# Six heads projected with the modulation, shift_m by stationary weights, latent attention beside the output product

## The chip, the cores and the metric

The kernel runs on one core of a Trainium2 chip. The metric is the device time of one execution in microseconds (us). Before the change the median of three runs is 2721.38 us (2719.5 to 2721.91).

## The reference, cut to what matters

Two transformer blocks work on 256 rows of width 2048. The change touches the first block up to the end of its output product:

```python
mod = silu(c) @ w_ada + b_ada                       # 2048 x 12288
shift_m, scale_m, gate_m, shift_f, scale_f, gate_f = split(mod, 6)
h = modulate(rmsnorm(x, g_norm_mix), shift_m, scale_m)
dq, dk, dv, q_lat, kv_lat, k_pe = split(h @ w_in)   # 8 heads x 384 columns, 512, 256, 64
o_diff = rmsnorm(softmax(q1 k1) v - lam * softmax(q2 k2) v, g_diff_sub) * 0.8   # 8 heads of 128
q = rmsnorm(q_lat, g_q_a) @ w_q_b                   # 8 heads x (128 + 64 rotated)
k_nope, v_mla = split(rmsnorm(kv_lat, g_kv_a) @ w_kv_b)   # 8 heads x (128, 128)
o_mla = softmax(q [k_nope, rope(k_pe)]) @ v_mla
x = x + gate_m * (concat(o_diff, o_mla) @ w_out)
h = modulate(rmsnorm(x, g_norm_ffn), shift_f, scale_f)    # the feed-forward part follows
```

Everything is float32. The feed-forward part of the block and the whole second block are untouched.

## The kernel before, in words

**The weight stream.** `make_plan` writes one list of tiles, each at most 128x1024 float32 (two row blocks by 512 columns; 384 KB for a difference head). SyncE's DMA queue loads them in the order of the list into 8 raw buffers (6, and 2 more; from block j = 2 of the output product on only the 6). `split_next` takes the next tile. A *main* tile, a weight of a matrix product, is split in two parts: ScalarE rounds the high part `wh` and VectorE forms the rest `wl` (both in `split`, L119 and L120). Four split tiles can wait (`ahead` says how many are wanted). A *side* tile is a piece of `w_ada`: it goes to `ada_part`, where VectorE multiplies it by silu(c) and sums along the row (L224). Only `shift_m` goes to TensorE there: two matmuls of 512 columns with one column of silu(c) as weights (L208) add to one row of 512 sums, and after 8 tiles ScalarE copies the row (L212) and four matmuls of one element (L215) turn it into a column.

**The products.** `linear` takes a split tile and issues 12 matmuls for it (`mm3`, L134 to L136: high by high, high by low, low by high, for two row blocks of the result and two row blocks of the weight). After each tile it ticks the *fillers*: generators with the attention heads' steps (and some others), of which a tick advances at most two. `ensure` and `drain` advance fillers with no product between them.

**The order of the first block.** `block1_attention_proj` takes the 2048 features in four quarters: the modulation of a quarter (8 tiles of `scale_m`, 8 of `shift_m`), then of that quarter q_lat, kv_lat and difference head 0, whose results stay in PSUM over all four quarters. Then head 1, q's and k/v's latent products (L573 to L627 with `cq_gen`, `ckv_gen`, `qr_gen`). `block1` then projects heads 2 to 7 while the steps of `mla_head` and `diff_head` run as fillers. It waits for all latent heads and four difference heads, splits their results into `OT`, and multiplies by w_out: blocks j = 0 and 1 with the first six of eight groups of features, the remaining attention, the last two groups, and then j = 2 and 3. Side tiles of `gate_m`, `scale_f` and `shift_f` are spread between: 24 over 28 main tiles, 48 over the next 48, and 8 over the last 22.

In `diff_head` the row norm of a head's result takes its reciprocal root on GpSimd (12 instructions of 128x1, L98 and L100); ScalarE then scales the result `on` (L736) and TensorE transposes it.

Of the kernel before, what the change touches and what calls it, by code (L numbers as in the profile page):

```python
# [42 lines left out]
class Kernel:  # L43
    def __init__(self, ctx, tc, a, out, offs):
# [9 lines left out]
        gap.tile([P, 88], F32, name="gap")  # L54
# [144 lines left out]
    def ada_part(self, e, src):  # L199

        v = self.nc.vector
        sec, k = e["sec"], e["k"]
        if e["kind"] == "ada_pe":
            if k == 0:
                self.ada_row = self.trp()
            for kk in range(2):
                kt = k * 2 + kk
                self.nc.tensor.matmul(self.ada_row[0:1, :], lhsT=self.silu_c[:, kt:kt + 1],  # L208
                                      rhs=src[:, kk * 512:(kk + 1) * 512], start=kt == 0, stop=kt == 15)
            if k == 7:  # L210
                row = self.junkp.tile([P, 512], F32, tag="junk", name="row")[0:1]
                self.nc.scalar.activation(row, self.ada_row[0:1, :], AF.Copy)  # L212
                ps = self.trp()
                for i in range(4):
                    self.nc.tensor.matmul(ps[:, i:i + 1], lhsT=row[:, i * P:(i + 1) * P], rhs=self.ones[0:1, 0:1],  # L215
                                          start=True, stop=True)
                c = slice(e["j"] * 4, e["j"] * 4 + 4)
                v.tensor_add(self.mod[sec][:, c], ps[:, 0:4], self.s("b_" + sec)[:, c])
                self.done.add((sec, e["j"]))
            return  # L220
        junk = self.adap.tile([P, 1024], BF16, tag="ajunk", name="ajunk", bufs=1)
        if k == 0:
            self.ada_sum = self.tiny("ada_sum", 8)
        v.scalar_tensor_tensor(junk, src, 1.0, self.silu_row[:, (k % 2) * 1024:(k % 2 + 1) * 1024],  # L224
                               op0=OP.mult, op1=OP.mult, accum_out=self.ada_sum[:, k:k + 1])
        if k == 7:
            c = slice(e["j"] * 4, e["j"] * 4 + 4)
            dst = self.mod[sec][:, c]
            h = self.ada_sum.rearrange("p (i h) -> p i h", h=2)
            v.tensor_add(dst, h[:, :, 0], h[:, :, 1])  # L230
            v.tensor_add(dst, dst, self.s("b_" + sec)[:, c])
            if sec.startswith("scale"):
                gain = self.s("g_norm_mix" if sec == "scale_m" else "g_norm_ffn")[:, c]
                v.scalar_tensor_tensor(dst, dst, 1.0, gain, op0=OP.add, op1=OP.mult)
            self.done.add((sec, e["j"]))
# [210 lines left out]
    def block1_attention_proj(self):  # L446
        nc, v = self.nc, self.nc.vector
        es = ExitStack()
        keep = es.enter_context(self.tc.tile_pool(name="mla", bufs=1))
        qn = keep.tile([P, 8, T], F32, name="qn")  # L450
        kn = keep.tile([P, 8, T], F32, name="kn")
        vm = keep.tile([P, 2, 1024], F32, name="vm")
        qr = keep.tile([P, 4, T], F32, name="qr")
        kr = keep.tile([P, 2, T], F32, name="kr")
        v.memset(kr, 0.0)
        pj0 = keep.tile([P, 2, 384], F32, name="pj0")
        pj1 = keep.tile([P, 2, 384], F32, name="pj1")
        sc = -float(192.0 ** -0.5)
        with ExitStack() as e2:
            tp = e2.enter_context(self.tc.tile_pool(name="lat", bufs=1))  # L460
            self.junkp = tp
            lat = {}

            def ql_():
                if "ql" not in lat:
                    lat["ql"] = tp.tile([P, 2, 512], F32, tag="ql", name="ql")
                return lat["ql"]
            kv = tp.tile([P, 2, 384], F32, name="kv")
            cq = self.hl_tile(tp, [P, 4, T], "cq")
            ckv = self.hl_tile(tp, [P, 2, T], "ckv")  # L470
            ssq = self.tiny("ssq", 2, bufs=1)
            ssk = self.tiny("ssk", 2, bufs=1)

            def ev_q(acc, tt):
                nc.scalar.activation(ql_()[:, tt], acc, AF.Copy)
                self.sumsq_chunk(acc, ssq[:, tt:tt + 1])

            def cq_gen():
                yield
                r = self.mean_rsqrt(ssq, 2, 512, "r_q")  # L480
                ql = lat["ql"]
                for tt in range(2):
                    v.tensor_scalar(ql[:, tt], ql[:, tt], r[:, tt:tt + 1], None, op0=OP.mult)
                yield
                for b in range(2):
                    ps = self.trp()
                    for i in range(2):
                        for tt in range(2):
                            self.T(ps[:, i * T + tt * P:i * T + (tt + 1) * P],
                                   ql[:, tt, (b * 2 + i) * P:(b * 2 + i + 1) * P])  # L490
                    for i in range(2):
                        kt = b * 2 + i
                        self.split(cq[:, kt], ps[:, i * T:(i + 1) * T], self.s("g_q_a", kt, kt + 1))
                self.done.add("cq")

            def ev_kv(acc, tt):
                nc.scalar.activation(kv[:, tt, 0:320], acc, AF.Copy)
                self.sumsq_chunk(acc[:, 0:256], ssk[:, tt:tt + 1])

            def ckv_gen():  # L500
                yield
                r = self.mean_rsqrt(ssk, 2, 256, "r_k")
                tmp = tp.tile([P, 2, 1, 64], F32, name="kr_tmp")
                for tt in range(2):
                    v.tensor_scalar(kv[:, tt, 0:256], kv[:, tt, 0:256], r[:, tt:tt + 1], None, op0=OP.mult)
                    self.rope(kv[:, tt, None, 256:320], self.cos_m[:, tt], self.sin_m[:, tt], 1, tmp)
                    v.tensor_copy(kv[:, tt, 320:384], kv[:, tt, 256:320])
                yield 3
                ps = self.trp()
                for i in range(2):  # L510
                    for tt in range(2):
                        self.T(ps[:, i * T + tt * P:i * T + (tt + 1) * P], kv[:, tt, i * P:(i + 1) * P])
                for kt in range(2):
                    self.split(ckv[:, kt], ps[:, kt * T:(kt + 1) * T], self.s("g_kv_a", kt, kt + 1))
                ps = self.trp()
                for tt in range(2):
                    self.T(ps[:, tt * P:(tt + 1) * P], kv[:, tt, 256:384])
                v.tensor_copy(kr[0:64, 0], ps[0:64, 0:T])
                v.tensor_copy(kr[64:128, 1], ps[64:128, 0:T])
                self.done.add("ckv")  # L520

            def ev_d(acc, tt):
                nc.scalar.activation(pj0[:, tt], acc, AF.Copy)

            for _ in range(6):
                self.split_next()
            self.lam()
            self.rope_tables(tp)
            for _ in range(8):
                self.split_next()  # L530
            ss = self.tiny("ss8", 8, bufs=2)
            for tt in range(2):
                for j in range(4):
                    self.sumsq_chunk(self.x[:, tt, j * 512:(j + 1) * 512], ss[:, tt * 4 + j:tt * 4 + j + 1])
            s2 = self.tiny("ssx", 2)
            v.tensor_reduce(s2, ss.rearrange("p (t j) -> p t j", t=2), axis=AX.X, op=OP.add)
            r = self.mean_rsqrt(s2, 2, D, "r_mix")
            A = self.new_A()
            jobs = [([self.acc(), self.acc()], 512, ev_q, cq_gen), ([self.acc(), self.acc()], 320, ev_kv, ckv_gen),
                    ([self.att(), self.att()], 384, ev_d, None)]  # L540

            def next_x(q):
                xh = tp.tile([P, 2, 512], F32, tag="ql", name="xh")
                hh = tp.tile([P, 4, T], F32, tag="rtmp", name="hh")
                self.x_hat(q, r, xh)
                for b in range(2):
                    nc.scalar.activation(hh[:, 2 * b:2 * b + 2], self.x_hat_T(b, xh), AF.Copy)
                return hh

            hh = next_x(0)  # L550
            for q in range(4):
                self.ahead = (3, 3, 3, 3)[q]
                self.run_ada(q)
                if q in (0,):
                    self.split_ahead()
                for b in (0, 2):
                    self.modulate(A, 4 * q + b, 2, hh[:, b:b + 2], "m", hh[:, b:b + 2])
                for i, (acc, w, ev, gen) in enumerate(jobs):
# [1176 lines left out]
```

## Time and profile before

| | us |
|---|---|
| median of three runs | 2721.38 |
| the profiled execution | 2718.8 |
| its span | 2717.1 |
| TensorE busy in the span | 2649.4 (98%) |
| VectorE busy | 1698.4 (63%) |
| ScalarE busy | 1245.6 (46%) |
| GpSimd busy | 83.2 (3%) |

The mean granted TensorE clock is 0.993 of full. The page cuts the span into 40 slices of 68 us; TensorE's busy share in tenths and the DMA's rate are, slice by slice:

```profile
PE   7999989899999999999999999999999999999999
PEclk9999999999999999999999999999999999999999
GB/s 368 327 268 270 267 255 275 244 231 236 237 238 235 218 192 193 186 161 159 252 127 100 159 178 187 186 192 192 186 189 188 191 193 188 192 192 189 192 191 151
```

The first block's attention and its output product fill the first seven slices (the product's last matmul ends at 478 us). Only there is TensorE's digit below 9. Busy is a share of time in which an engine has an instruction; a busy TensorE need not run at the full clock.

### The profile page before, as it was taken

What the parts mean: (1) busy time and instruction counts of PE and PEld (TensorE: products, weight loads), DVE (VectorE), ACT (ScalarE), POOL (GpSimd) and SP (SyncE); (2) the same over time, 40 slices, a digit from 0 to 9 for tenths busy, and PEclk for the clock granted to TensorE, in tenths of its full rate; (3) what the DMA queues carried; (4) which work ended last, traced back from release to release, by engine and by line L of the source; (5) the groups of instructions that cost most, each with busy time, mean ns of one, the idle gap of its engine ahead of it and who ended that gap; (6) DMA issues with size and microseconds to landing.
All of it is one profiled execution on the core that took longest, in us unless ns stands there. A gap on an engine that the chain in (4) does not pass through costs nothing.

```text
span 2717.1 us, 34409 instructions
## 1 busy us (share of the span) xinstructions
PE 2649.4 (98%) x12646; PEld 2218.6 (82%) x12646; DVE 1698.4 (63%) x2761; ACT 1245.6 (46%) x1791; POOL 83.2 (3%) x151
## 2 busy tenths in 40 slices
PE   7999989899999999999999999999999999999999
PEld 3588977688888888888898998888888888888887
DVE  5687977866666555667766665555554545454555
ACT  3255664344444444454655554444444344434443
POOL 0002320000000000002000000000000000000000
PEclk9999999999999999999999999999999999999999
DMA  9977777667777655545743555666566666666664
GB/s 368 327 268 270 267 255 275 244 231 236 237 238 235 218 192 193 186 161 159 252 127 100 159 178 187 186 192 192 186 189 188 191 193 188 192 192 189 192 191 151
DMA packets 163608, 568.85 MB, mean 209 GB/s; under 512 B 18288, under 2 KB 18544, under 8 KB 162800
## 3 DMA queue, kind: packets, MB, share of 16 engines
q1 hardware_dynamic: 160992, 558.70, 63.3%
q10 hardware_dynamic: 2448, 7.97, 0.8%
q8 instruction: 99, 1.62, 0.2%
q14 instruction: 69, 0.57, 0.1%
HBM read 564.50 MB, written 2.10 MB: 209 GB/s over the span
## 4 chain that ended last, share of the span: by engine, by line
PE 52%; DVE 1%; issue 0%; ACT 0%; DVEq 0%; ACTq 0%
PE acc L134 16%; PE acc L135 16%; PE acc L136 16%; PE tr L140 1%; PE at L1162 1%; DVE wl L120 0%; PE at L1159 0%; PE tr L1166 0%; ACT wh L119 0%; DVE jk L999 0%; PE at L1259 0%; PE at L1223 0%; PE at L1239 0%; PE at L1211 0%; PE at L1208 0%
## 5 line engine op out<-in xcount | busy, mean ns | idle before, releaser
L120 DVE TENSOR_TENSOR wl<-raw,wh 128x1024 fp32r<-128x1024 f32 (+3 forms) x926 | 1070.9, 1164 | 806.7 <-ACT wh L119 804.1
L119 ACT ACTIVATE wh<-raw 128x1024 fp32r<-128x1024 f32 (+3 forms) x926 | 930.5, 1010 | 961.1 <-PE acc L136 895.2
L134 PE MATMUL acc<-wh,Ah 128*128 128x512 f32 (+2 forms) x2400 | 912.8, 380 | 6.2 <-ACT Ah L119 4.5
L135 PE MATMUL acc<-wl,Ah 128*128 128x512 f32 (+2 forms) x2400 | 895.5, 373 | 9.3 <-DVE wl L120 9.3
L136 PE MATMUL acc<-wh,Al 128*128 128x512 f32 (+2 forms) x2400 | 894.8, 373 | 0.5 <-DVE Al L120 0.5
L134 PEld LDWEIGHTS acc<-wh,Ah 128*128 128x128 f32 x2400 | 454.4, 189 | 83.6 <-issue 10.2
L135 PEld LDWEIGHTS acc<-wl,Ah 128*128 128x128 f32 x2400 | 454.4, 189 | 76.9 <-DVE wl L120 12.6
L136 PEld LDWEIGHTS acc<-wh,Al 128*128 128x128 f32 x2400 | 453.7, 189 | 65.9 <-DVE Al L120 2.0
L224 DVE SCALAR_TENSOR_TENSOR ajunk<-raw,silu_row 128x1024 bf16<-128x1024 f32 x160 | 195.1, 1219 | 13.4 <-ACT silu_row L251 11.9
L134 PE MATMUL acc<-wh,midh 128*128 128x512 f32 x512 | 200.3, 391 | 0.5 <-ACT wh L119 0.3
L135 PE MATMUL acc<-wl,midh 128*128 128x512 f32 x512 | 199.5, 390 | 1.2 <-DVE wl L120 1.2
L136 PE MATMUL acc<-wh,midl 128*128 128x512 f32 x512 | 199.4, 389 | 0.0
L134 PE MATMUL acc<-wh,mid2h 128*128 128x512 f32 x352 | 137.4, 390 | 0.0
L136 PE MATMUL acc<-wh,mid2l 128*128 128x512 f32 x352 | 137.0, 389 | 0.0
L135 PE MATMUL acc<-wl,mid2h 128*128 128x512 f32 x352 | 137.0, 389 | 0.0
L135 PEld LDWEIGHTS acc<-wl,midh 128*128 128x128 f32 x512 | 96.2, 188 | 21.4 <-DVE wl L120 1.9
L134 PEld LDWEIGHTS acc<-wh,midh 128*128 128x128 f32 x512 | 96.1, 188 | 20.8 <-ACT wh L119 0.7
L136 PEld LDWEIGHTS acc<-wh,midl 128*128 128x128 f32 x512 | 96.1, 188 | 20.2 <-DVE midl L120 0.4
L136 PEld LDWEIGHTS acc<-wh,mid2l 128*128 128x128 f32 x352 | 66.1, 188 | 13.7
L134 PEld LDWEIGHTS acc<-wh,mid2h 128*128 128x128 f32 x352 | 66.1, 188 | 13.5
L135 PEld LDWEIGHTS acc<-wl,mid2h 128*128 128x128 f32 x352 | 66.1, 188 | 13.5
L135 PE MATMUL acc<-wl,O2h 128*128 128x512 f32 (+1 forms) x208 | 72.0, 346 | 0.3 <-DVE wl L120 0.3
(430 smaller groups left out, 2152.4 us busy)
## 6 DMA issues: line engine op xcount, KB each, us to landing
raw<-ff SPq DMA_DIRECT2D x256, 512.0 KB, 4.3
raw<-f2g SPq DMA_DIRECT2D x88, 512.0 KB, 3.7
raw<-f2u SPq DMA_DIRECT2D x88, 512.0 KB, 3.7
raw<-f2d SPq DMA_DIRECT2D x88, 512.0 KB, 3.7
raw<-wo SPq DMA_DIRECT2D x64, 512.0 KB, 4.3
raw<-wi_d SPq DMA_DIRECT2D x64, 384.0 KB, 4.6
raw<-w_fox SPq DMA_DIRECT2D x64, 384.0 KB, 3.6
raw<-ada_scale_m SPq DMA_DIRECT2D x32, 512.0 KB, 6.6
```

Source lines behind the costliest of these rows:

```text
L119: self.nc.scalar.activation(dst.hi, src, AF.Copy)
L120: self.nc.vector.tensor_sub(dst.lo, src, dst.hi.bitcast(F32))
L134: mm(out, lhsT=x.hi, rhs=w.hi, start=start, stop=False)
L135: mm(out, lhsT=x.hi, rhs=w.lo, start=False, stop=False)
L136: mm(out, lhsT=x.lo, rhs=w.hi, start=False, stop=stop)
L140: self.nc.tensor.transpose(out, in_, self.ident[0:n, 0:n])
L224: v.scalar_tensor_tensor(junk, src, 1.0, self.silu_row[:, (k % 2) * 1024:(k % 2 + 1) * 1024], op0=OP.mult, op1=OP.mult, accum_out=self.ada ...
L1162: mm(ps1, lhsT=qT[:, kb, P:T], rhs=kcat[:, g, kb].rearrange("p t b k -> p (t b k)"), start=kb == 0, stop=kb == 1)
```

## The change

1. **shift_m by stationary weights.** Its tiles are now laid out as those of the other sections. For each, eight blocks of 128x128 of the tile are the weights and a column of silu(c) is what moves (L209, one column each), into one column of a transposing buffer; ScalarE copies that column to `ada_col`, and VectorE ends the section as it does the others (`ada_end`).
2. **Six difference heads by quarters.** Heads 0 to 5 are projected with q_lat and kv_lat, quarter by quarter. Their partial results are added up in SBUF by VectorE (`part`), since PSUM has no room. Heads 6 and 7 follow whole. The steps of the difference heads run as fillers beside the last quarter and heads 6 and 7.
3. **Latent attention beside the output product.** The latent products come after all difference heads. The difference heads' results are split into `OT`, x is loaded, and the product begins with their features (four groups of j = 0 and 1); the steps of the latent heads run beside it, and `mla_head` splits its result straight into `OT`. `OT` is in memory of its own; the latent tiles lie in the buffers of A.
4. **The stream.** In each quarter the 16 side tiles are spread over the first 13 main tiles, and the 80 side tiles of the later sections evenly over all 58 main tiles from head 6 to the end of the output product.

The core of the diff:

```diff
-            if k == 0:
-                self.ada_row = self.trp()
-            for kk in range(2):
-                kt = k * 2 + kk
-                self.nc.tensor.matmul(self.ada_row[0:1, :], lhsT=self.silu_c[:, kt:kt + 1],
-                                      rhs=src[:, kk * 512:(kk + 1) * 512], start=kt == 0, stop=kt == 15)
+            ps = self.trp()
+            for kk in range(8):
+                kt = (k % 2) * 8 + kk
+                self.nc.tensor.matmul(ps[:, 0:1], lhsT=src[:, kk * P:(kk + 1) * P],
+                                      rhs=self.silu_c[:, kt:kt + 1], start=kk == 0, stop=kk == 7)
+            self.nc.scalar.activation(self.ada_col[:, k:k + 1], ps[:, 0:1], AF.Copy)
...
+        def part(dst, w, q):
+            def ev(acc, tt):
+                if q == 0:
+                    nc.scalar.activation(dst[:, tt, 0:w], acc, AF.Copy)
+                else:
+                    v.tensor_add(dst[:, tt, 0:w], acc, dst[:, tt, 0:w])
...
+        accq = [self.acc(), self.acc()]
+        pairs = [[self.acc(), self.acc()], [self.att(), self.att()]]
+        self.ahead = 3
+        make_h(0, next_x(0))
+        self.split_ahead()
+        for q in range(4):
+            xs = self.halves_of(A, range(q * 4, q * 4 + 4))
+            self.linear(xs, 512, ev_q, acc=accq, first=q == 0, last=q == 3)
+            if q < 3:
+                hh = next_x(q + 1)
+            else:
+                self.add(cq_gen())
+                O = self.xp.tile([P, 16, T], F32, tag="x", name="O")
+            for i in range(7):
+                acc = pairs[i % 2] if q < 3 else None
+                if i == 0:
+                    self.linear(xs, 320, part(kv, 320, q), acc=acc)
+                    if q == 3:
+                        self.add(ckv_gen())
+                    continue
+                h = i - 1
+                self.linear(xs, 384, part(pjs[h], 384, q), acc=acc)
+                if q == 3:
+                    self.add(self.diff_head(h, pjs[h], O, wp, kabs[h % 2]))
+                elif i == 5:
+                    make_h(q + 1, hh)
...
         yield 2
+        yield from self.wait_for("OT")
         po = self.att()
...
-        nc.scalar.activation(O[:, 8 + h], po[:, 0:T], AF.Copy)
+        self.split(OT["OT"][:, 8 + h], po[:, 0:T])
...
-        accs = [self.linear(pre, 512, None, last=False) for j in range(2)]
+        accs = [self.linear(groups[0:4], 512, None, last=False) for j in range(2)]
+        self.add(gm_gen())
+        self.ensure(*[("mla", h) for h in range(4)])
+        for j in range(2):
+            self.linear(groups[4:6], 512, None, acc=accs[j], first=False, last=False)
         self.drain()
...
-            plan += mix(part, mod(q + 1) if q < 3 else [], 1, 3)
+            plan += even(part[:13], mod(q + 1) if q < 3 else []) + part[13:]
...
-        plan += even(first[:28], side[:n1]) + even(first[28:76], side[n1:n1 + n2]) + even(first[76:], side[n1 + n2:])
+        plan += even(first, side)
```

How instructions stand against each other on an engine is shown at three places (line numbers are each kernel's own). First TensorE's queue from its start to the first matmuls of the q_lat product; `silu_c` is silu(c), `xh` the normed rows of x. Before:

```order
L248 MATMUL tr<-ident,silu_c 128x128 x16
L208 MATMUL tr<-raw,silu_c 1x512 x14
L140 MATMUL tr<-ident,xh 128x128 x8
L208 MATMUL tr<-raw,silu_c 1x512 x2
L215 MATMUL tr<-ones,row 128x1 x4
L208 MATMUL tr<-raw,silu_c 1x512 x6
L134 MATMUL acc<-wh,Ah 128x512
```

The same stretch after:

```order
L247 MATMUL tr<-ident,silu_c 128x128 x16
L209 MATMUL tr<-silu_c,raw 128x1 x56
L140 MATMUL tr<-ident,xh 128x128 x8
L209 MATMUL tr<-silu_c,raw 128x1 x16
L134 MATMUL acc<-wh,Ah 128x512
```

In place of 22 matmuls of 512 columns (11 tiles) and the four of L215 there are 72 of one column (9 tiles) ahead of the first product.

Second, ScalarE's queue around the last scaling of the first difference heads' results (`on<-on,r_d`, which waits for GpSimd's root `r_d`); `on<-at` (L729 before, L765 after) is the step before GpSimd's chain, and L655 and L741 are exponentials of a latent and of a difference head. Before:

```order
L119 ACTIVATE wh<-raw 128x768
L672 ACTIVATE O<-at 128x256
L637 ACTIVATE PT<-tr 128x512
L119 ACTIVATE wh<-raw 128x768
L736 ACTIVATE on<-on,r_d 128x128 x2
L655 ACTIVATE E,s<-at,nm 128x256 x2
L119 ACTIVATE wh<-raw 128x768
L741 ACTIVATE O<-tr,g_210 128x256
L729 ACTIVATE on<-at,r_2055 128x128 x2
L732 ACTIVATE jk,ssd<-on 128x128 x2
```

After:

```order
L765 ACTIVATE on<-at,r_2229 128x128 x2
L768 ACTIVATE jk,ssd<-on 128x128 x2
L741 ACTIVATE E,sd<-at,nmd 128x256 x4
L119 ACTIVATE wh<-raw 128x768
L672 ACTIVATE PT<-tr 128x512
L119 ACTIVATE wh<-raw 128x768
L772 ACTIVATE on<-on,r_d 128x128 x2
L119 ACTIVATE wh<-raw 128x768
L777 ACTIVATE O<-tr,g_238 128x256
L772 ACTIVATE on<-on,r_d 128x128 x2
L119 ACTIVATE wh<-raw 128x768
L777 ACTIVATE O<-tr,g_238 128x256
```

A latent head's steps stood between two difference heads before; after, the first two difference heads follow each other, with one split tile between their scalings.

Third, VectorE's queue ahead of the last evacuation of the output product (`gtmp<-acc,gm`); `ajunk` are side tiles, `wl` main tiles. Before:

```order
L224 SCALAR_TENSOR_TENSOR ajunk,ada_sum<-raw,silu_row 128x1024
L120 TENSOR_TENSOR wl<-raw,wh 128x1024 x2
L224 SCALAR_TENSOR_TENSOR ajunk,ada_sum<-raw,silu_row 128x1024
L230 TENSOR_TENSOR shift_f<-ada_sum 128x4
L231 TENSOR_TENSOR shift_f<-shift_f,small 128x4
L120 TENSOR_TENSOR wl<-raw,wh 128x1024
L224 SCALAR_TENSOR_TENSOR ajunk,ada_sum<-raw,silu_row 128x1024
L120 TENSOR_TENSOR wl<-raw,wh 128x1024
L224 SCALAR_TENSOR_TENSOR ajunk,ada_sum<-raw,silu_row 128x1024
L120 TENSOR_TENSOR wl<-raw,wh 128x1024
L797 TENSOR_TENSOR gtmp<-acc,gm 128x512
```

After:

```order
L218 SCALAR_TENSOR_TENSOR ajunk,ada_sum<-raw,silu_row 128x1024 x2
L120 TENSOR_TENSOR wl<-raw,wh 128x1024
L218 SCALAR_TENSOR_TENSOR ajunk,ada_sum<-raw,silu_row 128x1024
L120 TENSOR_TENSOR wl<-raw,wh 128x1024
L218 SCALAR_TENSOR_TENSOR ajunk,ada_sum<-raw,silu_row 128x1024 x2
L229 TENSOR_TENSOR shift_f<-ada_sum 128x4
L230 TENSOR_TENSOR shift_f<-shift_f,small 128x4
L120 TENSOR_TENSOR wl<-raw,wh 128x1024
L218 SCALAR_TENSOR_TENSOR ajunk,ada_sum<-raw,silu_row 128x1024
L120 TENSOR_TENSOR wl<-raw,wh 128x1024
L218 SCALAR_TENSOR_TENSOR ajunk,ada_sum<-raw,silu_row 128x1024
L120 TENSOR_TENSOR wl<-raw,wh 128x1024
```

Between the third evacuation of the product and its last, there were fewer side tiles than main tiles; now there are more. From the first evacuation to the last VectorE's queue holds 25 side tiles beside 18 main tiles after, against 8 beside 18 before.

## Rows read from the trace of the kernel before

**Rows 1.** Stretches: us, busy (x) by engine, PEclk, DMA share, GB/s
```profile
20.00:40.00 20.00, 14.61 (x43) 3.50 (x41) 15.16 (x50) 10.00 (x23) 0.00 (x0) 1.00 1.00 395
160.00:180.00 20.00, 15.57 (x81) 14.52 (x82) 19.20 (x48) 7.28 (x11) 0.00 (x0) 0.83 0.69 252
258.00:282.00 24.00, 19.73 (x101) 17.73 (x100) 18.32 (x40) 11.20 (x30) 6.62 (x8) 0.93 0.64 217
282.00:358.00 76.00, 75.22 (x425) 68.89 (x424) 67.76 (x152) 51.45 (x135) 30.39 (x48) 1.00 0.85 293
358.00:384.00 26.00, 19.43 (x83) 15.54 (x81) 20.00 (x44) 16.13 (x40) 3.45 (x12) 0.80 0.58 209
```

**Rows 2.** Groups by form, TensorE's L208: x, busy us, mean ns, idle before
```profile
L208 PE MATMUL tr<-raw,silu_c 128*1 128x512 f32 x128 | 58.7, 592 | 2.5 <-DMA raw<-ada_shift_m 2.5
```

**Rows 3.** TensorE's timeline, narrow matmuls: start us, us, operation, count
```profile
66.58 1.05 PE L215 MATMUL tr<-ones,row 1*128 1x1 f32 x8 [0.68 <-ACT row L212]
...
1386.67 0.96 PE L1166 MATMUL tr<-kcT,nqT 96*128 96x15 f32 x8
```

**Rows 4.** TensorE's waits from 20 to 520 us: in total, times, longest
```profile
PE tr L215 <- ACT row L212: 2.8, 4, 0.7
PE tr L140 <- ACT hh L547: 2.7, 4, 0.7
```

**Rows 5.** TensorE's timeline, the opening
```profile
32.80 1.88 PE L208 MATMUL tr<-raw,silu_c 128*1 128x512 f32 x4
...
44.99 0.50 PE L134 MATMUL acc<-wh,Ah 128*128 128x512 f32 x1 [2.70 <-ACT Ah L119]
```

**Rows 6.** TensorE's timeline, two waits that end a gathering
```profile
162.06 0.30 PE L140 MATMUL tr<-ident,kv 128*128 128x128 f32 x1 [3.17 <-DVE kv L505]
...
377.53 0.79 PE L134 MATMUL acc<-wh,Ah 128*128 128x512 f32 x1 [1.77 <-ACT Ah L119]
```

**Rows 7.** TensorE's timeline, two of one run of 384-column matmuls
```profile
150.22 0.33 PE L135 MATMUL acc<-wl,Ah 128*128 128x384 f32 x1
...
151.26 0.33 PE L135 MATMUL acc<-wl,Ah 128*128 128x384 f32 x1
```

**Rows 8.** TensorE's timeline, difference heads' last products and transposes of `on`
```profile
235.87 1.16 PE L725 MATMUL at<-pj,PT 128*128 128x128 f32 x8 [0.79 <-ACT E L705]
...
250.44 0.62 PE L140 MATMUL tr<-ident,on 128*128 128x128 f32 x2 [0.72 <-ACT on L736]
...
264.87 0.62 PE L140 MATMUL tr<-ident,on 128*128 128x128 f32 x2 [4.12 <-ACT on L736]
```

**Rows 9.** GpSimd's timeline: first and last of a head's chain, twice
```profile
240.38 5.97 POOL L98 TENSOR_SCALAR rs_t<-r_d,rs_h 128x1 f32<-128x1 f32 x2 [238.95 <-DVE rs_h L92]
...
249.69 0.51 POOL L100 TENSOR_SCALAR r_d<-rs_t,r_d 128x1 f32<-128x1 f32 x2
...
373.15 0.70 POOL L98 TENSOR_SCALAR rs_t<-r_d,rs_h 128x1 f32<-128x1 f32 x2 [16.44 <-DVE rs_h L92]
...
376.10 0.50 POOL L100 TENSOR_SCALAR r_d<-rs_t,r_d 128x1 f32<-128x1 f32 x2
```

**Rows 10.** VectorE's timeline in the output product
```profile
405.36 1.22 DVE L224 SCALAR_TENSOR_TENSOR ajunk<-raw,silu_row 128x1024 bf16<-128x1024 f32 x1
...
406.50 1.22 DVE L120 TENSOR_TENSOR wl<-raw,wh 128x1024 fp32r<-128x1024 f32 x1
...
426.72 0.69 DVE L797 TENSOR_TENSOR gtmp<-acc,gm 128x512 f32<-128x512 f32 x1
...
456.06 0.68 DVE L797 TENSOR_TENSOR gtmp<-acc,gm 128x512 f32<-128x512 f32 x1
...
458.72 1.22 DVE L224 SCALAR_TENSOR_TENSOR ajunk<-raw,silu_row 128x1024 bf16<-128x1024 f32 x1
...
477.83 0.68 DVE L797 TENSOR_TENSOR gtmp<-acc,gm 128x512 f32<-128x512 f32 x1
```

**Rows 11.** TensorE's timeline, its first work after the output product
```profile
484.89 2.00 PE L140 MATMUL tr<-ident,xh 128*128 128x128 f32 x8 [6.62 <-issue]
```

More of the change, by code (lines that the diff above doesn't have):

```diff
@@ L53, in __init__ @@
         gap = pool("gap", 1)
-        gap.tile([P, 88], F32, name="gap")
+        gap.tile([P, 56], F32, name="gap")
         self.sm = pool("sm", 4)
@@ L204, in ada_part @@
             if k == 0:
-                self.ada_row = self.trp()
-            for kk in range(2):
-                kt = k * 2 + kk
-                self.nc.tensor.matmul(self.ada_row[0:1, :], lhsT=self.silu_c[:, kt:kt + 1],
-                                      rhs=src[:, kk * 512:(kk + 1) * 512], start=kt == 0, stop=kt == 15)
-            if k == 7:
[L211 to L219, printed above, removed]
+                self.ada_col = self.tiny("ada_col", 8)
+            ps = self.trp()
[4 more added lines that the diff above has]
+            self.nc.scalar.activation(self.ada_col[:, k:k + 1], ps[:, 0:1], AF.Copy)
+            if k == 7:
+                self.ada_end(e, self.ada_col)
             return
@@ L444, in lam, with block1_attention @@
         nc.vector.tensor_scalar(self.g08, self.s("g_diff_sub"), 1.0 - 0.2, None, op0=OP.mult)
-    def block1_attention_proj(self):
+    def block1_attention(self):
         nc, v = self.nc, self.nc.vector
         es = ExitStack()
[L449 to L457, printed above, removed]
-        sc = -float(192.0 ** -0.5)
[L459 to L508, printed above, removed]
@@ new lines, in block1_attention @@
+        wp = es.enter_context(self.tc.tile_pool(name="wp1", bufs=1))
+        self.junkp = wp
+        kabs = []
+        for i in range(2):
+            k = wp.tile([P, 2, T], F32, name=f"kab{i}")
+            v.memset(k, 0.0)
+            kabs.append(k)
+        sc = -float(192.0 ** -0.5)
+        e2 = ExitStack()
+        tp = e2.enter_context(self.tc.tile_pool(name="lat", bufs=1))
+        cq = self.hl_tile(tp, [P, 4, T], "cq")
+        ckv = self.hl_tile(tp, [P, 2, T], "ckv")
+        pjs = [tp.tile([P, 2, 384], F32, name=f"pj{i}") for i in range(8)]
@@ new lines, in block1_attention, with ev_q, cq_gen @@
+        kv = tp.tile([P, 2, 384], F32, name="kv")
+        lat = {}
+        ssq = self.tiny("ssq", 2, bufs=1)
+        ssk = self.tiny("ssk", 2, bufs=1)
+        def ev_q(acc, tt):
+            if "ql" not in lat:
+                lat["ql"] = tp.tile([P, 2, 512], F32, tag="ql", name="ql")
+            nc.scalar.activation(lat["ql"][:, tt], acc, AF.Copy)
+            self.sumsq_chunk(acc, ssq[:, tt:tt + 1])
+        def cq_gen():
+            yield
+            r = self.mean_rsqrt(ssq, 2, 512, "r_q")
+            ql = lat["ql"]
+            for tt in range(2):
+                v.tensor_scalar(ql[:, tt], ql[:, tt], r[:, tt:tt + 1], None, op0=OP.mult)
+            yield
+            for b in range(2):
@@ L535, in block1_attention_proj @@
[L535 to L558, printed above, removed]
-                    self.linear(self.halves_of(A, range(q * 4, q * 4 + 4)), w, ev, acc=acc, first=q == 0, last=q == 3)
-                    if q == 3 and gen:
-                        self.add(gen())
-                    if i == 0 and q < 3:
-                        hh = next_x(q + 1)
@@ new lines, in block1_attention @@
+        self.ahead = SPLIT_BUFS
+        allk = self.halves_of(A, range(16))
+        for h in (6, 7):
+            pj = pjs[h]
+            def ev_d(acc, tt):
+                nc.scalar.activation(pj[:, tt], acc, AF.Copy)
+            self.linear(allk, 384, ev_d)
+            self.add(self.diff_head(h, pj, O, wp, kabs[h % 2]))
+        X, Y = [self.ap_.tile([P, 16, T], F32, tag=t, name=t + "m") for t in ("Ah", "Al")]
+        qn, kn = X[:, 0:8], X[:, 8:16]
+        vm = Y[:, 0:8].rearrange("p (a b) t -> p a (b t)", a=2)
@@ L608, in block1_attention_proj @@
[L608 to L617 removed]
+                    self.tick()
@@ L631, in p_transpose_evac @@
+            for h in range(half * 4, half * 4 + 4):
+                self.add(self.mla_head(h, mla, OT, wp), 1 + h % 4)
+        self.ahead = SPLIT_BUFS
+        self.ensure(*[("diff", h) for h in range(8)])
+        e2.close()
+        return es, O, OT, wp
     def p_transpose_evac(self, blocks, dst, n):
@@ L1643, in layout @@
                                        for h in range(s, s + 4)]) for s in (0, 4)], 1)
[L1644 to L1645 removed]
+    A["wo"] = pack(L("w_out"), chunks(4, 512), 2)
     A["ff1"] = pack(L("w_ff1"), chunks(16, 512), 2)
```

271 lines of the change are left out of this document (144 added, 127 removed).

## The prediction, made before the changed kernel was run

> **What bounds the kernel now.** I read the page's busy shares first: TensorE is busy 98% of the span, so what can change is its idle time, its clock and its own work. The slices put nearly all idle time into the first 500 us, where the changed code runs. I then read that part by stretches. In three of them TensorE is short of work and its clock is below full: 160 to 180, 258 to 282 and 358 to 384 us [rows 1]. They lose 4.43, 4.27 and 6.57 us of idle time (length less TensorE's busy time), and clock besides: the time that a granted share below one costs is (1 - share) times the length, 3.4, 1.7 and 5.2 us, part of which is idle time counted twice. The waits name the cause: `kv` being normed and rotated on VectorE for 3.17 us [rows 6], the reciprocal root of a difference head on GpSimd, for which TensorE waits 4.12 us through ScalarE's `on` [rows 8], and the gathering of eight latent and four difference heads before the output product, whose last wait is 1.77 us [rows 6]. After the product TensorE waits 6.62 us more [rows 11].
>
> **The change part by part.** Matmuls of the products, transposes and attention are as many as before, up to the end of the output product; only the order differs. So the sum is over the shift product and over the waits.
>
> *a. The shift product.* Removed are 58.7 us of L208 [rows 2] and, four times, 1.05 of L215 [rows 3], 62.9 us. Added are 32 tiles of eight one-column matmuls, of which each shows two records. No row has a 128x128 float32 weight with one moving column. The nearest are L215 (one row, one column: 8 records in 1.05 us) and L1166 (96 rows, 15 columns: 8 records in .96 us) [rows 3]. A tile has 16 records, twice a row's: at most 2.10 or 1.92 us, and less by the overlap where two rows would join, .15 us, an estimate from one row's eighth. That is 1.95 by L215 and 1.77 by L1166, 62.4 or 56.6 us in all. The upper bound takes no overlap: 32 x 2.10 = 67.2. Neither is nearer by its shape (L215 in the columns, L1166 in the wide weight); I take their middle, 59.5: **-3.4**, between -6.3 and +4.3.
>
> *b. Waits in the quarters.* TensorE waits 2.8 us for ScalarE's row copy and 2.7 for `hh` [rows 4]. The row is gone, and `hh` is made five linear products ahead. What is new is a copy of [128,1] per tile behind ScalarE's splits; two transposing buffers cover it by one tile. About 2 of 5.5 us stay: **-3.5** (-5.5 to +2).
>
> *c. The opening.* The first product starts at 44.99 us after a wait of 2.70 [rows 5]. After, two shift tiles fewer stand ahead of it (3.8 us by rows 5, they come later), and the wait depends on the same DMA and modulation. I gain the part of the wait that the deferred work left open: **-1.5** (-3 to 0).
>
> *d. The hole at 160 to 180 us.* The step that norms `kv` now runs beside the last quarter's difference heads, six tiles or more ahead of who needs it. 4.43 us of idle time and 3.4 of clock go [rows 1]; the alternating accumulators, which wait for VectorE's addition, take .5 back: **-7.3** (-8 to -3).
>
> *e. The difference heads' roots.* From a head's last product to the transpose of `on` before: 235.87 to 250.44, 14.57 us, of which GpSimd's twelve instructions take 240.38 to 250.20, 9.8 us [rows 8, 9]. Before, TensorE waited 4.12 + .72 for the first two heads, with 1.7 us of clock and .3 that the stretch has beside: 6.9 us go. After, eight heads have this chain beside a running product. Their cover, by the order, is for heads 0 to 5 four 384-column tiles with another head's steps: a tile is 12 x (151.26 - 150.22)/6 = 2.08 us [rows 7], the steps some 17 narrow matmuls of .25 us (1.16 us for 4, [rows 8], less the last one's overhang), together 12.5 us. Heads 0 and 1 follow each other by one split tile on ScalarE's queue, and GpSimd works in order: the second waits for the first. Their two waits: 14.57 - 12.5 = 2, and some 5 behind it; heads 2 to 6 have covers of 12.5 to 14.8 against a mean chain of 12.9, about 1 each at the most and mostly none, 2 in all; head 7 has the steps of latent products only, 9.4 us, and waits 3.5; with clock 2 and 1 for uneven tiles, 15.5: **+8.6** (-1 to +20). The waiting `on` stands ahead of a `wh` split in ScalarE's order, so a late root also holds back the tiles after it; three or four ready tiles, 6 to 8 us of products, cover that.
>
> Here the trace and a rule speak against the change. The same twelve instructions took 9.8 us while VectorE split tiles and only 3.45 (373.15 to 376.60) while VectorE had little to do [rows 9]. The Trainium skill says why in "SBUF — State Buffer", section "Who interferes with whom": a VectorE instruction with two SBUF inputs and a GpSimd access exclude each other, and one blocks while the other runs. The trace agrees in direction. The splits and side tiles both have two SBUF inputs. By the rule, all eight chains would be as long as the longest; the rival below takes that from rows.
>
> *f. The gathering before the product.* Between 358 and 384 us 6.57 us idle and part of 5.2 of clock go, 9.5 in all [rows 1, 6]. In its place `OT`'s first split (about 1.5 us, by 1.77 in rows 6) and the latent heads' scores and exponentials where no product tile is between, 2.5: **-5.5** (-9 to +3).
>
> *g. Heads 6 and 7.* VectorE has there, with 22 side tiles and 16 splits beside two heads' steps, 55.6 us of work against TensorE's 55: **+1.5** (0 to +5).
>
> *h. The tail of the product.* From the first evacuation (426.72) to TensorE's restart (484.89) are 58.2 us. VectorE's queue there now has 25 side tiles in place of 8, with the 18 splits as before. A side tile takes 1.14 us in a run (405.36 to 406.50), a split has the same duration (1.22), an evacuation of two row blocks 2.66 (456.06 to 458.72) [rows 10]: 25 x 1.145 + 18 x 1.14 + 3 x 2.66 + 1.4 of small ones = 58.5, and from the last evacuation to the restart 484.89 - 477.83 = 7.06, as before [rows 10, 11]. That is 65.6 in place of 58.2: **+7.4**. The DMA must bring 43 tiles of .524 MB in that time, 386 GB/s less what waits in the buffers, and it has shown 395 [rows 1]. The range is +3 (three or four tiles split ahead) to +12 (the DMA ends last).
>
> The sum: -3.4 - 3.5 - 1.5 - 7.3 + 8.6 - 5.5 + 1.5 + 7.4 = -3.7. The profiled execution took 2718.8 us, of which 1.7 lie around its span; with the sum 2715.1. The median of the runs is 2.6 above the profiled execution: **2718**.
>
> **The rivals.**
>
> 1. *The heads are covered better* and the product's tail finds tiles split ahead: e at +1.5, h at +4: 10.5 us less, about **2707**. For it: in 282 to 358 us, between the low stretches, TensorE is busy 75.22 of 76 us beside the same heads [rows 1]. Against: there a latent head's steps lay between two difference heads.
>
> 2. *GpSimd's chain decides* (slower). Every head's chain lasts 14.57 us or more, since VectorE is fuller: 25 side tiles' worth of two-input work where it was 8. Eight heads at 14.57 - 12.5 = 2, with the second of a pair waiting a whole chain (9.8) more, come to 30 in place of 15.5: +14, **2732**. It decides from a cover below the chain, which holds for the first pair already. For it: 9.8 against 3.45 us [rows 9]. Against: most chains later were 7 to 9 us, and VectorE's queue stalls there leave gaps.
>
> 3. *The clock falls under the one-column matmuls.* In 160 to 180 us the clock stood at .83 of full where TensorE had been short of work, that is, it went between 2.4 and 1.2 GHz [rows 1]. Each such fall cost 2 to 3 us. One per quarter and one at the start give +11, **2729**. For it: no row shows the clock beside a long run of such matmuls. Against: the low stretches of the trace follow idle time, none of them narrow work [rows 1].
>
> 4. *The order does not do what it says*: the DMA or VectorE bounds the stages anyhow, and the gains of d and f are waited off elsewhere: -3.7 + 7.3 + 5.5 = +9, about **2730**; VectorE is busy 63% over all, against it.
>
> **How the numbers follow.** My forecast, 2712 to 2724, has a chance of .42; rival 1 (2701 to 2712) .22; rival 2 (2724 to 2740) .22; rival 3 .09; rival 4 .05. The unknown of a alone makes 10 us of width, that of e 20 and that of h 9; together the range that holds 8 of 10 is 2701 to 2738, the forecast's own is 2712 to 2724. Within .2% (5.4 us, about what a measurement of this kernel can tell from no change) is 2716.0 to 2726.8. Below it lie rival 1 and .18 of the forecast's .42: .40. Above it most of rival 2 (.17), rivals 3 and 4 together .12: .29. The rest is .31.
>
> **What would show it.** a: L209's rows take about 1.86 us a tile, 59 to 60 in all, at a full clock. d: no wait of TensorE for `kv`. e: waits of TensorE for `on` of some 10 us between the end of the third quarter and the latent products, each ending at GpSimd's last root. f: the first w_out matmul follows the latent products within 2 us. h: VectorE busy without a gap over the last 55 us of the product, and its last evacuation some 7 us later, counted from the first, than before. What would make the prediction wrong: a fall of the clock in the quarters, waits for tiles (`wh`, `wl`) there, or latent heads whose steps hold back the product.

## The result and the profile after

The changed kernel takes 2761.68 us (median of four runs, 2757.36 to 2768.71) against 2720.55 before: 1.0153 times as long, interval 1.0131 to 1.0175. The forecast was 2718, the range ended at 2738. The profiled span is 2759.3 us, 42.2 more than before. From TensorE's restart after the output product to the end both take 2232 us, so all of it lies in the changed part: the first product starts 8.5 us later (53.49 for 44.99 [rows 5]); from there to the product's first evacuation it takes 21.8 us more (to 457.02, for 426.72 [rows 10]); from there to the restart 12.0 more (to 527.22, for 484.89 [rows 11]). VectorE's first evacuation and TensorE's restart after the change:

```profile
457.02 0.69 DVE L805 TENSOR_TENSOR gtmp<-acc,gm 128x512 f32<-128x512 f32 x1
```

```profile
527.22 2.00 PE L140 MATMUL tr<-ident,xh 128*128 128x128 f32 x8 [11.16 <-issue]
```

Stretches of the changed kernel, with the columns of [rows 1]:

```profile
20.00:40.00 20.00, 13.37 (x63) 13.28 (x63) 8.91 (x34) 9.49 (x25) 0.00 (x0) 0.50 0.85 322
40.00:60.00 20.00, 14.92 (x57) 12.89 (x58) 14.27 (x40) 5.83 (x10) 0.00 (x0) 0.54 0.41 123
60.00:180.00 120.00, 118.45 (x730) 114.56 (x729) 67.36 (x110) 41.73 (x77) 0.00 (x0) 0.92 0.76 271
212.00:260.00 48.00, 39.29 (x191) 33.65 (x190) 36.10 (x107) 23.02 (x47) 0.00 (x0) 0.93 0.37 114
260.00:345.00 85.00, 71.80 (x387) 62.93 (x386) 78.14 (x195) 51.66 (x146) 42.70 (x64) 0.94 0.75 256
457.00:527.00 70.00, 53.97 (x218) 42.31 (x216) 64.78 (x111) 24.11 (x34) 0.00 (x0) 0.90 0.89 327
```

Three things are to be seen. In the opening the granted clock is half, 1.2 of 2.4 GHz; before it was full. In the first three quarters TensorE has no gap to speak of, while VectorE is busy 56%. Beside the difference heads (260 to 345) and in the product's tail VectorE is nearly full, 92 and 93% busy, and TensorE waits. Its waits from 200 to 400 us (us in total, times, longest) name many things:

```profile
PE tr L140 <- ACT on L772: 9.6, 5, 3.4
PE at L761 <- ACT E L741: 6.2, 2, 5.1
PE acc L135 <- DVE wl L120: 4.7, 2, 3.9
PE at L733 <- ACT kab L726: 2.8, 1, 2.8
```

The longest of them can be followed back to VectorE. TensorE had a head's scores ready at 328.93 us (L733). VectorE takes their row minima (`nmd`, L734), which ScalarE needs for the exponentials `E`. It comes to them only at 334.36, behind three side tiles (`ajunk`, the first at 328.78) and two `wl`. ScalarE starts `E` at 335.07, and TensorE has waited 5.12 us. Rows of VectorE, ScalarE and TensorE:

```profile
328.78 1.22 DVE L218 SCALAR_TENSOR_TENSOR ajunk<-raw,silu_row 128x1024 bf16<-128x1024 f32 x1
...
333.22 1.22 DVE L120 TENSOR_TENSOR wl<-raw,wh 128x1024 fp32r<-128x1024 f32 x1
334.36 1.27 DVE L734 TENSOR_REDUCE nmd<-at 128x2 f32<-128x512 f32 x2
```

```profile
335.07 0.47 ACT L741 ACTIVATE E<-at,nmd 128x256 f32<-128x256 f32 x1 [3.32 <-DVE nmd L734]
```

```profile
327.05 1.88 PE L733 MATMUL at<-kab,qT 128*128 128x512 f32 x4
...
336.14 2.08 PE L761 MATMUL at<-pj,PT 128*128 128x128 f32 x8 [5.12 <-ACT E L741]
```

TensorE's timeline of the opening:

```profile
12.61 3.63 PE L209 MATMUL tr<-silu_c,raw 128*128 128x1 f32 x32
16.78 16.59 PE L209 MATMUL tr<-silu_c,raw 128*128 128x1 f32 x80 [0.54 <-DMA raw<-ada_shift_m]
42.84 2.06 PE L140 MATMUL tr<-ident,xh 128*128 128x128 f32 x8 [9.47 <-DVE xh L407]
44.73 6.98 PE L209 MATMUL tr<-silu_c,raw 128*128 128x1 f32 x32
53.49 0.80 PE L134 MATMUL acc<-wh,Ah 128*128 128x512 f32 x1 [1.77 <-ACT wh L119]
```

Two tiles take 3.63 us at full clock, the next five 16.59, most of it at half. Then TensorE idles 9.47 us for the normed rows. ScalarE's timeline shows why they are late: the first of eight sums of squares of x (L401) starts only behind the seventh copy of `ada_col`, which waited for TensorE; before, it started at 21.31. After, then before:

```profile
33.41 0.17 ACT L211 ACTIVATE ada_col<-tr 128x1 f32<-128x1 f32 x1 [3.24 <-PE tr L209]
33.47 0.62 ACT L401 ACTIVATE junk<-x 128x512 f32<-128x512 f32 x1
```

```profile
21.31 0.61 ACT L402 ACTIVATE junk<-x 128x512 f32<-128x512 f32 x1
```

In the last quarter VectorE norms and rotates `kv` from 236.65 to 241.34 us, and a main tile's `wl` stands behind it. VectorE's rows, then the matmul that waited:

```profile
241.24 0.20 DVE L509 COPY kv<-kv 128x64 f32<-128x64 f32 x1
241.34 0.95 DVE L120 TENSOR_TENSOR wl<-raw,wh 128x768 fp32r<-128x768 f32 x1
```

```profile
242.35 0.44 PE L135 MATMUL acc<-wl,Ah 128*128 128x384 f32 x1 [3.90 <-DVE wl L120]
```

### The profile page after: what moved, and what is told of

Same layout as the page of the kernel before. It is cut to its first block, busy times and chain, and to the rows that moved or that the text cites. A ratio compares the mean times of both kernels' runs of the same rounds, so it can differ in the third digit from the quotient of the medians.

```text
span 2759.3 us, 35205 instructions
## 1 busy us (share of the span) xinstructions
PE 2670.3 (97%) x12998; PEld 2287.5 (83%) x12998; DVE 1720.3 (62%) x2812; ACT 1246.1 (45%) x1816; POOL 84.5 (3%) x151
## 4 chain that ended last, share of the span: by engine, by line
PE 51%; DVE 1%; ACT 0%; issue 0%; DVEq 0%; ACTq 0%
PE acc L134 16%; PE acc L135 16%; PE acc L136 16%; PE tr L140 1%; PE at L1171 0%; DVE wl L120 0%; PE at L1168 0%; PE tr L1175 0%; ACT wh L119 0%; DVE jk L1008 0%; PE at L1232 0%; PE at L1268 0%; PE at L1248 0%; PE at L1220 0%; PE at L1217 0%
## 5 line engine op out<-in xcount | busy, mean ns | idle before, releaser
L120 DVE TENSOR_TENSOR wl<-raw,wh 128x1024 fp32r<-128x1024 f32 (+2 forms) x926 | 1071.1, 1164 | 829.9 <-ACT wh L119 827.1
L119 ACT ACTIVATE wh<-raw 128x1024 fp32r<-128x1024 f32 (+2 forms) x926 | 929.1, 1011 | 944.5 <-PE acc L136 873.8
L134 PE MATMUL acc<-wh,Ah 128*128 128x512 f32 (+2 forms) x2232 | 846.6, 379 | 4.3 <-ACT wh L119 4.2
L135 PE MATMUL acc<-wl,Ah 128*128 128x512 f32 (+2 forms) x2232 | 835.1, 374 | 12.4 <-DVE wl L120 12.1
L136 PE MATMUL acc<-wh,Al 128*128 128x512 f32 (+2 forms) x2232 | 833.5, 373 | 0.0
L135 PEld LDWEIGHTS acc<-wl,Ah 128*128 128x128 f32 x2232 | 424.5, 190 | 75.8 <-DVE wl L120 17.0
L134 PEld LDWEIGHTS acc<-wh,Ah 128*128 128x128 f32 x2232 | 424.8, 190 | 65.2 <-ACT wh L119 5.4
L136 PEld LDWEIGHTS acc<-wh,Al 128*128 128x128 f32 x2232 | 424.1, 190 | 58.7 <-DVE Al L120 0.2
L209 PEld LDWEIGHTS tr<-silu_c,raw 128*128 128x128 f32 x512 | 74.7, 230 | 2.3 <-ACT hh L539 1.7
```

Source lines behind the costliest of these rows:

```text
L119: self.nc.scalar.activation(dst.hi, src, AF.Copy)
L120: self.nc.vector.tensor_sub(dst.lo, src, dst.hi.bitcast(F32))
L134: mm(out, lhsT=x.hi, rhs=w.hi, start=start, stop=False)
L135: mm(out, lhsT=x.hi, rhs=w.lo, start=False, stop=False)
L136: mm(out, lhsT=x.lo, rhs=w.hi, start=False, stop=stop)
L209: self.nc.tensor.matmul(ps[:, 0:1], lhsT=src[:, kk * P:(kk + 1) * P], rhs=self.silu_c[:, kt:kt + 1], start=kk == 0, stop=kk == 7)
```

## The experiments

"Restart" is TensorE's first work after the output product in the profiled execution (before 484.89, changed 527.22).

**1. shift_m by rows in the changed order** (`ada_part` and the tiles' layout of the kernel before).

> The changed kernel with shift_m as before: two matmuls of 512 columns per tile into one row, the row copied and turned. All else as changed. Theory A (the one-column matmuls take TensorE to the low clock in the opening and once per quarter, and their copies stand in ScalarE's queue ahead of the sums of squares): the opening's first product falls from 53.5 to 43-47 us, the clock between 20 and 60 us is 1.0, three low stretches in the quarters go, 4 us of matmul time come back: 2739 to 2747 us. Rival B (the low clock comes of the order of the quarters and not of these matmuls): the first product stays after 50 us and the time at 2757 to 2766.

2772.77 us. The opening did what A says (first product 40.88 us, clock 1.00 from 20 to 40 and 0.91 from 40 to 60), and the restart came at 518.66, 8.6 us earlier. But from the restart to the end it took 2250 us in place of 2232. So the total, above both ranges, does not judge A; the runs under 3 and 4 explain it.

**2. The new shift_m alone in the kernel before.**

> The kernel before with only shift_m by one-column matmuls, in its layout. Theory A: the opening is 8 to 12 us later, each quarter's transposes and burst lose 2 us, less 4 us of matmul time: 2730 to 2738 us. Rival B: 2716 to 2720, the 4 us saved.

2766.33 us, restart 513.40, and again 2252 us behind it. The changed kernel balances its new tile `ada_col` (8 columns, four buffers, 32 columns in all) with a `gap` tile of 56 in place of 88 columns. after_rows lost `ada_col` and before_cols won it, and neither changed the gap. So, by these sizes, all pools laid out later lay 32 columns, 128 bytes a partition, lower in the one and higher in the other.

**3. and 4. The same two with the gap that fits.**

```diff
-        gap.tile([P, 56], F32, name="gap")      # after_rows2
+        gap.tile([P, 88], F32, name="gap")
```

> As after_rows, and the gap tile back at 88 columns, as the kernel before has with this shift_m: ada_col's 32 columns are gone, so that all later pools lie again where they lay. Theory G (matmul spacing depends on where the pools lie in SBUF): from TensorE's restart after the output product to the end 2232 us, as in the kernels before and after, in place of 2250; matmul spacing of 512 columns .2267 again; 2744 to 2751 us. Rival H (the shift product's form slows the rest, or the slower spacing is that run's own): 2768 to 2775.

> As before_cols, and the gap tile at 56 columns, as the changed kernel has beside ada_col. Theory G: restart to end 2232 us in place of 2252, in all 2739 to 2748 us, and what is left over the kernel before, 19 to 27, is theory A's: low clock and ScalarE's queue in the opening and the quarters. Rival H: 2760 to 2768.

2751.29 and 2746.51 us; restart to end 2231 and 2232. G holds (the first time is a third of a us above its range). A matmul's spacing, in the runs of after_rows and of after_rows2:

```profile
2000.09 0.40 PE L135 MATMUL acc<-wl,Mh 128*128 128x512 f32 x1
2000.33 0.40 PE L136 MATMUL acc<-wh,Ml 128*128 128x512 f32 x1
...
2001.95 0.40 PE L134 MATMUL acc<-wh,Mh 128*128 128x512 f32 x1
```

```profile
1999.91 0.39 PE L135 MATMUL acc<-wl,Mh 128*128 128x512 f32 x1
2000.13 0.39 PE L136 MATMUL acc<-wh,Ml 128*128 128x512 f32 x1
...
2001.72 0.39 PE L134 MATMUL acc<-wh,Mh 128*128 128x512 f32 x1
```

Eight steps are 1.86 us in the first, 1.81 in the second. What remains is A's, the clock and ScalarE's queue together: by columns the shift costs 10 us in the new order (2761.7 - 2751.3) and 26 in the old (2746.5 - 2720.6). In the old order four tiles in place of two stand between the transposes and the first product, which starts 16.4 us later than in the kernel before (61.36 for 44.99), and the granted clock from 60 to 180 us is 0.81. before_cols2:

```profile
44.43 13.81 PE L209 MATMUL tr<-silu_c,raw 128*128 128x1 f32 x64
61.36 0.80 PE L134 MATMUL acc<-wh,Ah 128*128 128x512 f32 x1 [3.11 <-ACT Ah L119]
```

**5. ScalarE's queue or the clock?** The sums of squares are issued ahead of the first tiles.

> The changed kernel with the sums of squares of x issued ahead of the first tiles, so that they stand in ScalarE's queue before the copies of ada_col. Theory Q (of the opening's loss, the larger part is ScalarE's queue: the sums wait behind copies that wait for TensorE at the low clock): the transposes of xh start at 33 to 35 us, when the burst of seven tiles ends, in place of 42.8, the first product at 44 to 47 in place of 53.5: 2751 to 2755 us. Rival R (the low clock alone sets it; the transposes move ahead but the rest of the modulation ends as late): first product 51 to 54, 2758 to 2764.

2758.63 us; first product 51.02. These are R's numbers: the idle time before the transposes goes, but they start only 2.4 us earlier, behind a burst that is still at half clock (0.50 from 20 to 40 us). The run does not part the two cleanly, though. The copies now stand behind the sums, and TensorE waits 3.11 us for one of them and 3.50 us more for a tile's DMA. Without these 6.6 us the transposes would start at 33.9, as Q has it (an estimate from the rows below). So the shares of the clock and of the queue stay open. Together they make 12.7 us of the opening (first product 53.49, in after_rows2 40.83).

```profile
19.75 10.40 PE L209 MATMUL tr<-silu_c,raw 128*128 128x1 f32 x48 [3.11 <-ACT ada_col L211]
33.65 6.96 PE L209 MATMUL tr<-silu_c,raw 128*128 128x1 f32 x32 [3.50 <-DMA raw<-ada_shift_m]
40.47 1.95 PE L140 MATMUL tr<-ident,xh 128*128 128x128 f32 x8
```

**6. GpSimd's roots.** `mean_rsqrt(ss, 2, 128, "r_d", True)` in `diff_head` without `True`.

> The changed kernel with the difference heads' reciprocal root on VectorE in place of GpSimd, 12 instructions of 128x1 a head. Theory E (GpSimd's chain is what `on` is waited for): the 9.6 us of TensorE's waits for `on` fall under 3, with some clock: 2750 to 2756 us. Rival F (VectorE's own queue is late there, and takes 8 times some 2.4 us more): 2758 to 2770, the waits moving to `wl`.

2772.72 us, 11 more than changed and 3 above F's range. GpSimd's chain is no longer there and the waits are, for `E` more than for `wl`:

```profile
PE at L761 <- ACT E L741: 12.0, 2, 7.0
PE tr L140 <- ACT on L772: 7.2, 2, 5.1
```

The variant gives work to the engine that is nearly full. It shows that the root is no better there, not that GpSimd's chain costs nothing.

**7. and 8. Where the side tiles stand.** The first moves them from the tail to the stages before; the second moves `gate_m`'s to the quarters (it also has a second tile of sums and a gap of 24 columns to balance it, and its restart to end is 2232 us).

```diff
-        plan += even(first, side)
+        plan += even(first[:40], side[:72]) + even(first[40:], side[72:])      # after_front
...
-            plan += even(part[:13], mod(q + 1) if q < 3 else []) + part[13:]
+            plan += even(part[:13], even(mod(q + 1), ada("gate_m", [q])) if q < 3 else ada("gate_m", [q])) + part[13:]  # after_early
```

> The changed kernel with 72 of the 80 later side tiles spread over the 40 main tiles ahead of the product's last 18, and 8 over those 18 (25 before). Theory C (the tail of the product is bound by VectorE's and the DMA's side tiles): from the first evacuation to TensorE's restart 58 to 62 us in place of 70.2, and 2749 to 2755 us. Rival D (the load is only moved, and the difference heads' stage is VectorE-bound): the tail is shorter but the stage before it longer by as much, 2757 to 2765.

> The changed kernel with the 32 side tiles of gate_m among the quarters' main tiles, eight to a quarter, in place of after them; 48 side tiles are left for the 58 main tiles from head 6 on. Theory V (VectorE is full from 260 to 345 us and, with the DMA, in the product's tail, while it has a third of its time free in the quarters): VectorE has 10 us less in each of those two stretches; the tail from first evacuation to restart 60 in place of 70 us, the heads' stage 6 to 10 us shorter: 2741 to 2749. Rival W (these stages are bound by the chains of the heads' own steps and the DMA's tail, and the quarters get longer): 2756 to 2766.

after_front: 2761.73 us, as D has it: the tail 56.0 us in place of 70.2, its start 11.3 later, the median unchanged. after_early: 2736.48 us, V's, and more: 25 us less. The stretch beside the heads, first of after_front, then of after_early:

```profile
260.00:345.00 85.00, 68.18 (x344) 59.81 (x345) 79.99 (x191) 47.13 (x136) 41.43 (x61) 0.88 0.80 279
```

```profile
260.00:345.00 85.00, 79.01 (x464) 70.30 (x464) 74.59 (x193) 57.10 (x157) 43.34 (x72) 0.98 0.67 228
```

With VectorE at 88 in place of 92 to 94% TensorE is busy 79.0 us where it was 68.2 to 71.8. Only side tiles moved, the heads' instructions are the same: VectorE's queue, more than any one chain, bounded the stage. GpSimd's part of a head took 5.4 to 7.7 us in place of 6.4 to 9.6, so some of the gain may have come through it.

**9. shift_m on VectorE**, by `kind = "ada"` for all sections. The new layout that VectorE's form needs is left out, so shift_m's values differ; instructions and sizes are those of the form.

> The changed kernel with shift_m on VectorE, as the other sections are. Theory V and A together: TensorE has 59 us less, VectorE 37 more in the first 210 us, where it has the room; first product at 40 to 45 us at full clock, a quarter 40 to 43 us (VectorE or the DMA ends it) in place of 52: 2712 to 2724. Rival W: VectorE has no room once its additions and splits stand between, a quarter takes 50 us and the gain is only the opening: 2743 to 2752.

2727.55 us, between the two. The first product comes at 45.84 us, but at half clock: TensorE idles 24.29 us ahead of it for the normed rows. The first three quarters shrink from 54 to 45 us on the mean, and VectorE ends them. It is 92% busy; TensorE's waits there are mostly for `wl`, and the DMA queue, at .91, waits 82 of the 120 us for VectorE to free raw buffers.

```profile
60.00:180.00 120.00, 103.08 (x536) 93.17 (x534) 110.62 (x190) 45.17 (x64) 0.00 (x0) 0.97 0.91 334
```

**10. to 13. The order with all that put right.** best1 has rows, the right gap, `gate_m` in the quarters and the other 48 side tiles as 4, 34 and 10. best2 also puts the roots of q_lat and kv_lat on GpSimd. best3 takes the side tiles from the last quarter, best4 keeps one tile more ahead there.

> The changed order with shift_m by rows (gap as fits), gate_m's 32 side tiles in the quarters, and the other 48 spread 4 over heads 6 and 7, 34 over the latent products and the product's first blocks, 10 over the last 18 main tiles. Theory V: the gains of after_rows2 (10), of after_early (25) and 6 to 10 more of the tail add up: restart at 485 to 491 us, 2717 to 2724. Rival W: the stage of the heads is bound by its own chains, and what is taken from the tail comes back in the blocks before: 2725 to 2733.

> best1 with the reciprocal roots of q_lat and kv_lat on GpSimd and the norm and rotation of kv_lat in two steps with a tick between. Theory K (in the last quarter VectorE's queue holds 4.7 us of kv_lat's chain ahead of a split, for which TensorE waits 3.9 us and loses clock): the waits for `wl` between 220 and 260 us go, 3 to 6 us less than best1. Rival: GpSimd's roots are so slow beside VectorE that cq and ckv are later and nothing is gained: within 2 us of best1 or above.

> best1 with no side tiles in the last quarter: gate_m's other 24 in the first three quarters, its last 8 among the latent products and the product's first blocks (42 there in place of 34). Theory V2 (what is left, 17 us of idle time and clock between 200 and 260 us, is VectorE: additions, kv_lat's chain, the heads' rotations and 8 side tiles in one quarter): 9 us of VectorE work leave that stretch, 4 to 8 us less: 2718 to 2723 us. Rival X (the waits there are the chains' own, each behind ScalarE and TensorE in turn): 2725 to 2729.

> best3 with four split tiles kept ahead in the last quarter in place of three. V2 and a stock of one more tile (2.1 us) against waits of up to 3.5 us for `wl`: 1 to 3 us less than best3, 2716 to 2722. Rival X: as best3.

2726.78, 2732.80, 2728.23 and 2724.95 us: 1.0024 (1.0015 to 1.0034), 1.0047, 1.0028 and 1.0020 (1.0011 to 1.0029) times the kernel before. None beats it. best1 is W's: 10 and 25 us add up, the 6 to 10 more do not come. best2's rival holds (head 7's wait for `on` is 5.63 us, cq no earlier). best3 is X's; best4 stands 3 us below it, but their intervals overlap. best3 shows where the rest is. The last quarter, then 313 to 342 us with most of the latent products, of best1 and of best3:

```profile
201.00:261.00 60.00, 47.24 (x223) 39.57 (x221) 50.30 (x142) 27.23 (x59) 0.00 (x0) 0.91 0.50 166
...
313.00:342.00 29.00, 27.35 (x180) 24.41 (x179) 24.79 (x58) 19.12 (x51) 17.52 (x32) 1.00 0.80 278
```

```profile
201.00:261.00 60.00, 50.40 (x248) 42.23 (x247) 46.23 (x138) 30.12 (x66) 0.00 (x0) 0.94 0.36 114
...
313.00:342.00 29.00, 24.14 (x152) 21.35 (x150) 25.01 (x53) 17.17 (x41) 17.74 (x24) 0.94 0.83 291
```

TensorE has three us more work done in the quarter and three less from 313 to 342. The latent products begin 5.4 us earlier (313.36 for 318.74), and yet the first w_out matmul comes at 369.7 to 369.8 us in both.

## Why the prediction was wrong

By stretch, the forecast was -1.5 for the opening (c), roughly -9.6 from the first product to the first evacuation (a, b, d to g) and +7.4 behind it (h). Measured were +8.5, +21.8 and +12.0. Two steps failed above all. For the opening I took a full clock and no new wait in ScalarE's queue under the one-column matmuls. The difference heads (e, g) I priced by single chains and by sums of work that came out level, where VectorE's full queue delays the chains. Rivals 3 and 4 had named both causes, but each alone, at 2729 and 2730 with chances of .09 and .05. Rival 4 was set aside because VectorE is busy 63% of the whole span, an average; where the side tiles stand it is 92%. Both came true together.

- **a**, the price of the shift product, was right: 1.8 us a tile at full clock, 59 in all for 62.9. But at the clock that was granted L209's rows came to 73.2 us.
- **c**, the opening, failed most plainly: -1.5 forecast, +8.5 measured, and -4.2 without the one-column matmuls (after_rows2). Rival 3 named the cause and mis-sized it: a fall was priced at 2 to 3 us; here the half clock lasted from 17 to 58 us. I also never placed the new copies in ScalarE's queue, where they stand ahead of the sums of squares.
- **b**: the waits for the row went (-2.8), but in each of the three quarters the clock fell behind the transposes and a shift tile (0.92 on the mean from 60 to 180 us, 0.99 in after_rows2), a loss I had left to rival 3. Most of it is one long fall, from 168 to 181 us; after_front and after_dvers, with the same quarters, do not have it (0.97).
- **d**: TensorE no longer waits for `kv` directly, yet the same VectorE chain now delays a split (3.90 us). From 212 to 260 us 8.7 us idle: the hole moved. The -7.3 itself was too much, since it adds a low clock to the idle time in which that clock cost nothing.
- **e**: "waits for `on` of some 10 us" came out (9.6), mostly by luck. Only two of the five, of 2.3 and 3.4 us, end at GpSimd's last root; in the others the root was there, and ScalarE came to `on` late behind other work. GpSimd's eight chains took 6.4 to 9.6 us, all below the 9.8 before, so rival 2, with every chain as long as the longest or longer, did not come true (the 25 side tiles that it counts are the tail's, not the heads'). after_early points to VectorE's queue, for which `E` and `wl` wait too.
- **g** was mis-sized: 55.6 against 55 us of work was read as +1.5. From 260 to 345 us VectorE was busy 78.1 and TensorE 71.8 of 85 us: level sums did not keep either full, since each waits for the other at times (`E`, 5.12 us). No run parts g from e. Moving 32 side tiles away (after_early) gained 25 us: 10.7 between the last quarter's start and the first w_out matmul, 10.9 in h's tail.
- **h**: +12.0 for +7.4, the end of its range; the mechanism was right (after_front: 14 us shorter with 8 side tiles).
- **f**: the first split's wait was right (1.21 us for 1.5), but before the product TensorE still idled 7.2 us from 345 to 390, 3.4 of them for head 7's `on`, where 6.57 were to go.

In all: of 41 us, some 10 are the shift product's form (after_rows2) and 25 the side tiles' places (after_early); best1, with both undone, stands 6 above the kernel before. Why these 6 remain is open. In best1 TensorE idles 12.8 us from 201 to 261 and 6.0 from 345 to 390, against 15.3 in the three stretches that the change was to remove [rows 1], and best3 shows that what is taken from one gap can show up in the next.

## What to carry to other kernels

Place every new instruction in the queue of each engine it enters, cheap ones too: a 0.17 us copy that waited for TensorE held back the sums of squares behind it. Before moving work, add up each engine's work by stage, not over the span: VectorE was 63% busy over all, 56% in the stages that could have taken the side tiles and 92% where they were put. When a variant changes any tile's size, compare a stretch that it cannot touch before reading the total.

## What the runs showed of the hardware

A shift of the later SBUF pools by 128 bytes a partition, down in after_rows and up in before_cols, made 512-column matmuls 2 to 3% slower in the stretch shown, and 18 to 20 us over 2232 us at full granted clock. Every run of either kernel is slower than every run of the same kernel with the gap that fits. Why was not tried.

The one-column float32 matmuls with 128x128 weights were followed by a fall to half clock in the opening in each kernel that had them there, though TensorE was busy without a gap from 7 to 16 us; the same stretch with L208 kept the full clock. In after_front the fall came between 15 and 16 us (granted clock 0.73 there, 0.50 behind it), within 56 such matmuls without a gap:

```profile
13.24 21.98 PE L209 MATMUL tr<-silu_c,raw 128*128 128x1 f32 x112
```

One such tile between products, as at 89.72, 93.59 and 105.77 us of the changed kernel, left the clock full (1.00 from 70 to 110).
